# Masking attention blocks with an identity matmul and two exponentials instead of GpSimd selects, in a two-layer hybrid decoder

## The chip, the cores and the metric

The kernel runs on one core of one Trainium2 chip. The metric is the device time of one execution in microseconds (us); the time before is the median of three runs.

## The reference

Two layers are applied to a prompt group (one sequence of 1024 tokens) and to a sample group (8 sequences with 4 new tokens each, with cached keys and values). Layer 0 projects the input to queries, keys, values and gates; an attention A (window 128, with a sink) and an attention B (three head groups with dilations 1, 4 and 16, merged by their softmax denominators) follow; the result is multiplied by a SiLU gate, projected and normalised. Layer 1 is an mLSTM and takes no part in the change. Cut to the attention over blocks of 128 queries:

```python
def banded_attention(q, k, v, span, sink=None):
    ...
    s = jnp.einsum('nbqhgd,nbkhd->nbhgqk', qb, kk, preferred_element_type=F32)
    qi = jnp.arange(BLOCK)[:, None] + BLOCK
    ki = jnp.arange(2 * BLOCK)[None, :]
    dist = qi - ki
    band = (dist >= 0) & (dist <= span)
    ...
    p, den, lse = _softmax_stats(s, mask, sink_b)
    o = jnp.einsum('nbhgqk,nbkhd->nbqhgd', p, vv.astype(F32))

def layer0_prompt(x, w_in, sinks, w_out, ln_g, ln_b):
    ...
    oa, _ = banded_attention(qa, ka, va, A_WINDOW, sinks.reshape(A_KV_HEADS, A_GROUP))
    ...
    for g in range(N_B_GROUPS):
        win, dil = B_DILATIONS[g]
        o, lse = banded_attention(_to_sub(qb[:, :, g], dil), _to_sub(kb[:, :, g], dil),
                                  _to_sub(vb[:, :, g], dil), win // dil)
    ...
    y = _layer0_out(x, oa, obs, lses, z, w_out, ln_g, ln_b)
```

## The kernel before

Matrix products are made from pairs: a number is split into a rounded part (F32R, `hi`, a copy on ScalarE, L111) and the rest (`lo`, a subtraction on VectorE, L114), and a product is three matmuls. Layer 0 runs in stages: keys and values (`proj_kv`), queries of attention A, then query projections of B woven with attention A and the row maxima of B (`weave`, L941), then the gate projections `proj_z0` (tile `pj`, L199 to L201) woven with attention B (L964), then what is left of attention B woven with the sample attention and the merges (L984), then the output projection `out0` (tile `py`, L165 to L167) and layer 1.

`scores` (L450) handles one block of 128 queries of 4 heads against 128 keys, as a tile of 128 keys x 512. There are 100 such blocks: 30 in attention A, 35 for each of the two key heads of attention B. Two matmuls fill a PSUM bank `sc` (L462, L463; the second one takes the low part of the query and the negative row maximum); ScalarE writes p = exp(sc) (L465); GpSimd puts zeros where a key must not be seen (L468 to L476: one select for the own or the previous block, two selects and a memset for the group with dilation 16); ScalarE copies p to the rounded `ph` (L479, counted under L112), and `pl` = p - ph is made on VectorE (L483, counted under L116) or, for every fourth block outside of attention A, on GpSimd (L481). Three matmuls `av` (L485 to L487) add the block to the output, which VectorE takes out (L577 to L580). `Q1` and `Q2` are loaded for every 256 queries, and ScalarE copies 64 rows of `Q1` to `Q2` (L370).

Instructions are put in order by a scheduler that simulates the engines; `ahead` gives a stream priority. Tiles live in pools whose memory is used again after a release, and a tile that takes over memory waits for the last reader of what was there. Two pools matter here. `sm` (L913) holds small tiles of the attention, the mask `maskq` first; it is released at L970, before the remaining blocks of attention B (those after `EARLY` = 9 steps of the second key head, called the late attention here) are written out. `smt` (L982, 4 buffers) is opened after that release and holds the tiles `KT`: all cached keys and values of the sample attention, 24 loads. Its first buffer takes over memory that `sm` had. All these loads are issued by SyncE (SP), which works its queue off in order, as are the loads of the Q tiles, of the output weights (`wr<-in_wo`, L848) and of the merges (`mo`, `mf`, `mz`, L830 to L832). The sample attention makes scores `sS` (L681) from `KT`, then `so` (L728) from `KT` and the weights. The output projection adds its result to `xr` (L879), loaded at L874.

## Time and profile before

| what | value |
|---|---|
| median of three runs | 1497.61 us (1493.66 to 1716.2) |
| the profiled execution's own time | 1500.81 us |
| its span on the core | 1499.1 us |
| mean granted TensorE clock | 0.973 of full |
| busy TensorE (PE) | 1405.4 us, 94% |
| busy VectorE (DVE) | 901.5 us, 60% |
| busy ScalarE (ACT) | 515.1 us, 34% |
| busy GpSimd (POOL) | 276.0 us, 18% |

The rows come from the one profiled execution. A matmul's recorded duration overlaps with the next one's, so the distance of two starts is what a matmul costs in a row of them. A busy share is a mean over stages that have different limits; the stages are looked at by windows of time. "a <- b" after an idle time names what the engine waited for.

### The profile page before, as it was taken

The page shows a single profiled execution, that of the slowest core. Times are in us where ns is not written, and L with a number is a line of the kernel's source. Part 1 is how long each engine was busy: PE and PEld are TensorE (multiplying, and loading weights), DVE is VectorE, ACT ScalarE, POOL GpSimd, SP SyncE. Part 2 cuts the span into 40 slices and gives each one's busy share as a digit, 9 for nine tenths or more (in the row PEclk, how much of TensorE's full clock was granted, in tenths as well). Part 3 has the DMA queues.
Part 4 walks back from the last instruction along what each step waited for, and adds up shares of the span by engine and source line. Part 5 has one row for each costly group of instructions (what it writes and reads, how often), then busy time and mean ns, then how long its engine had stood idle before and what let it go on. Part 6 is the DMA issues. An engine that isn't in the chain of part 4 may idle for free.

```text
span 1499.1 us, 21984 instructions
## 1 busy us (share of the span) xinstructions
PE 1405.4 (94%) x7792; PEld 1191.7 (79%) x7792; DVE 901.5 (60%) x2479; ACT 515.1 (34%) x938; POOL 276.0 (18%) x351
## 2 busy tenths in 40 slices
PE   8999999998899778979999999999999999999997
PEld 7989999898898444458788878988898899877785
DVE  5411457578566858768764536655565565566786
ACT  5332244542123776621133313331333133333310
POOL 1002233422322866401000000100000000000010
PEclk9999999999999888989999999999999999999999
DMA  8445655556653766794212655354223312431731
GB/s 307 168 142 171 199 190 164 173 162 185 186 190 111 195 169 186 241 300 140 95 51 87 220 191 201 109 194 124 78 82 122 108 50 69 131 116 39 233 131 46
DMA packets 139307, 226.86 MB, mean 151 GB/s; under 512 B 17216, under 2 KB 107296, under 8 KB 138680
## 3 DMA queue, kind: packets, MB, share of 16 engines
q1 hardware_dynamic: 131134, 204.09, 44.5%
q10 hardware_dynamic: 8064, 21.37, 4.0%
q8 instruction: 62, 1.02, 0.3%
q14 instruction: 47, 0.39, 0.1%
HBM read 166.60 MB, written 81.88 MB: 166 GB/s over the span
## 4 chain that ended last, share of the span: by engine, by line
PE 69%; DMA 16%; DVE 8%; issue 3%; ACT 2%; POOL 2%; SPq 1%; DVEq 0%; ACTq 0%; POOLq 0%
PE pj L199 10%; PE pj L201 10%; PE pj L200 10%; PE py L165 4%; PE py L167 3%; PE py L166 3%; DMA G<-GR 3%; PE pvo L165 3%; PE pvo L166 3%; PE pvo L167 3%; DMA wr<-in_wo_dram 1%; PE st L433 1%; DMA QZ<-QQ 1%; DMA out_cmems_dram<-Cs 1%; PE sc L463 1%
## 5 line engine op out<-in xcount | busy, mean ns | idle before, releaser
L199 PE MATMUL pj<-xh,wh 128*128 128x384 f32 (+1 forms) x576 | 189.3, 329 | 8.1 <-DVE sz L613 3.6
L199 PE MATMUL pj<-x1h,wh 128*128 128x384 f32 (+1 forms) x576 | 189.5, 329 | 1.7 <-ACT QT L1152 1.6
L200 PE MATMUL pj<-xl,wh 128*128 128x384 f32 (+1 forms) x576 | 188.5, 327 | 0.0
L201 PE MATMUL pj<-xh,wl 128*128 128x384 f32 (+1 forms) x576 | 188.4, 327 | 0.0
L201 PE MATMUL pj<-x1h,wl 128*128 128x384 f32 (+1 forms) x576 | 187.6, 326 | 0.0
L200 PE MATMUL pj<-x1l,wh 128*128 128x384 f32 (+1 forms) x576 | 187.4, 325 | 0.0
L199 PEld LDWEIGHTS pj<-xh,wh 128*128 128x128 f32 x576 | 110.6, 192 | 12.7 <-DVE sz L613 4.5
L199 PEld LDWEIGHTS pj<-x1h,wh 128*128 128x128 f32 x576 | 108.5, 188 | 6.5 <-issue 3.3
L201 PEld LDWEIGHTS pj<-x1h,wl 128*128 128x128 f32 x576 | 108.4, 188 | 6.0 <-issue 5.8
L200 PEld LDWEIGHTS pj<-xl,wh 128*128 128x128 f32 x576 | 110.5, 192 | 1.6
L201 PEld LDWEIGHTS pj<-xh,wl 128*128 128x128 f32 x576 | 110.8, 192 | 1.1
L200 PEld LDWEIGHTS pj<-x1l,wh 128*128 128x128 f32 x576 | 108.5, 188 | 4.0 <-issue 3.8
L437 DVE CUSTOM_DVE_ANT_0 junk<-st,maskq 128x256 f32<-128x256 f32 (+1 forms) x256 | 93.1, 364 | 27.4 <-PE st L433 6.8
L165 PE MATMUL pvo<-voh,x1h 128*128 128x512 f32 x256 | 101.0, 397 | 2.6 <-DVE SZ L1168 2.6
L166 PE MATMUL pvo<-voh,x1l 128*128 128x512 f32 x256 | 100.3, 394 | 0.0
L167 PE MATMUL pvo<-vol,x1h 128*128 128x512 f32 x256 | 99.7, 393 | 0.0
L807 POOL TENSOR_TENSOR rsw<-rsw,mhalf 128x1 f32<-128x1 f32 (+1 forms) x54 | 40.0, 741 | 322.3 <-DVE rsw L806 306.6
L116 DVE TENSOR_TENSOR pl<-p,ph 128x512 fp32r<-128x512 f32 x82 | 67.0, 825 | 29.0 <-ACT ph L112 27.0
L122 POOL TENSOR_TENSOR wl<-wr,wh 128x1024 fp32r<-128x1024 f32 x24 | 57.9, 2414 | 130.1 <-ACT qs L233 69.9
L112 ACT ACTIVATE wh<-wr 128x1024 fp32r<-128x1024 f32 x48 | 50.7, 1056 | 73.9 <-PE pj L200 69.6
L112 ACT ACTIVATE ph<-p 128x512 fp32r<-128x512 f32 x100 | 60.7, 627 | 27.0 <-POOL p L474 9.3
L1198 POOL MEMSET V<- 128x2 f32 x64 | 4.3, 99 | 348.6 <-PE num L1327 213.9
(350 smaller groups left out, 3244.8 us busy)
## 6 DMA issues: line engine op xcount, KB each, us to landing
Q<-QQ SPq DMA_DIRECT2D x32, 512.0 KB
out_kvs_dram<-in_cache_b_kv_dram SPq DMA_DIRECT2D x16, 1022.0 KB
wr<-in_w0f_dram SPq DMA_DIRECT2D x24, 512.0 KB
wr<-in_w1f_dram SPq DMA_DIRECT2D x24, 512.0 KB
QQ<-sh ACTq DMA_DIRECT2D x16, 512.0 KB
QQ<-sl ACTq DMA_DIRECT2D x16, 512.0 KB
QZ<-QQ SPq DMA_DIRECT2D x32, 256.0 KB
wr<-in_wo_dram SPq DMA_DIRECT2D x16, 512.0 KB
```

The source lines that it names most:

```text
L112: return self.nc.scalar.activation(out, in_, AF.Copy, scale=scale)
L116: return self.nc.vector.tensor_tensor(out, in_, f(hi), OP.subtract)
L122: self.nc.gpsimd.tensor_tensor(out, in_, f(hi), OP.subtract)
L165: nc.tensor.matmul(ps, xh[:, k, t], wh, start=k == 0, stop=False)
L166: nc.tensor.matmul(ps, xl[:, k, t], wh, start=False, stop=False)
L167: nc.tensor.matmul(ps, xh[:, k, t], wl, start=False, stop=k == 7)
L199: nc.tensor.matmul(ps[:, :n], wh[:, k, :], xh[:, k, :n], start=k == 0, stop=False)
L200: nc.tensor.matmul(ps[:, :n], wh[:, k, :], xl[:, k, :n], start=False, stop=False)
L201: nc.tensor.matmul(ps[:, :n], wl[:, k, :], xh[:, k, :n], start=False, stop=k == 7)
L433: nc.tensor.matmul(st[:, u, :], Q1[:, h, q0:q0 + 128], K1[:, w0:w0 + 256], start=True, stop=True)
L437: nc.vector.tensor_tensor_reduce(junk[:, :n], st[:, u, c0:c0 + n], mk, 1.0, -3e38, OP.add, OP.max, ST[:, 8 * h + qb:8 * h + qb + 1])
L807: nc.gpsimd.tensor_tensor(r, v, self.mhalf[:m], OP.pow)
```

## The change

A block's scores get a third matmul, ahead of the others: the mask (128 x 128, rounded values) as weights against `ident4`, four identity matrices side by side, puts the mask into the bank, and the two others add to it. The selects and the memset on GpSimd are gone. ScalarE makes the exponential of the bank twice, once rounded to `ph` and once in full to `p`; the copy from p to ph is gone. `p` has 3 buffers in place of 4. The mask comes through a buffer of the weights and a rounding copy to `maskr`, and `ident4` is made once on VectorE; both lie in `sm`.

```diff
--- before.py
+++ after.py
@@ -459,24 +459,15 @@
                 self.nsc += 1
                 ks = slice(128 * kb, 128 * kb + 128)
                 so = sc.rearrange("p (h q) -> p h q", h=4)
-                nc.tensor.matmul(so, K1[:, ks], Q1[:, :, q0:q0 + 128], start=True, stop=False)
+                mk = self.maskr[:, 256:384] if g == 3 else self.maskr[:, 128 - 128 * kind:256 - 128 * kind]
+                nc.tensor.matmul(so, mk, self.ident4, start=True, stop=False)
+                nc.tensor.matmul(so, K1[:, ks], Q1[:, :, q0:q0 + 128], start=False, stop=False)
                 nc.tensor.matmul(so, K2[:, ks], Q2[:, :, q0:q0 + 128], start=False, stop=True)
-                p = self.ppool.tile([128, 512], F32, tag="p", name="p", bufs=4)
-                nc.scalar.activation(p, sc, AF.Exp)
-                if g == 3:
-                    pv = p.rearrange("p (h s q) -> p h s q", h=4, s=2)
-                    nc.gpsimd.affine_select(pv[:, :, 0, :], pv[:, :, 0, :], [[0, 4], [1, 64]], OP.is_ge, 0.0,
-                                            base=0, channel_multiplier=-1)
-                    nc.gpsimd.affine_select(pv[:, :, 1, :], pv[:, :, 1, :], [[0, 4], [1, 64]], OP.is_ge, 0.0,
-                                            base=64, channel_multiplier=-1)
-                    nc.gpsimd.memset(pv[0:64, :, 1, :], 0.0)
-                elif kind == 0:
-                    nc.gpsimd.affine_select(p, p, [[0, 4], [1, 128]], OP.is_ge, 0.0, base=0, channel_multiplier=-1)
-                else:
-                    nc.gpsimd.affine_select(p, p, [[0, 4], [-1, 128]], OP.is_ge, 0.0, base=0, channel_multiplier=1)
                 ph = self.ppool.tile([128, 512], F32R, tag="ph", name="ph")
                 pl = self.ppool.tile([128, 512], F32R, tag="pl", name="pl")
-                self.hi(ph, p)
+                p = self.ppool.tile([128, 512], F32, tag="p", name="p", bufs=3)
+                nc.scalar.activation(ph, sc, AF.Exp)
+                nc.scalar.activation(p, sc, AF.Exp)
                 if g and self.nsc % POOL_LO == 0:
                     nc.gpsimd.tensor_tensor(pl, p, f(ph), OP.subtract)
                 else:
@@ -911,8 +902,14 @@
                 tc.tile_pool(name="vp", bufs=2) as self.vp, tc.tile_pool(name="ppool", bufs=3) as self.ppool, \
                 tc.tile_pool(name="odp", bufs=1) as self.odp:
             sm = self.sm = tc.alloc_tile_pool(name="sm", bufs=1)
-            self.maskq = self.sm.tile([128, 384], F32, name="maskq")
-            self.load(self.maskq, A['maskq'])
+
+            raw = self.wraw.tile([128, 1024], F32, tag="wraw", name="mkr")
+            self.load(raw[:, 0:384], A['maskq'])
+            self.maskr = self.sm.tile([128, 384], F32R, name="maskr")
+            self.hi(self.maskr, raw[:, 0:384])
+            self.maskq = f(self.maskr)
+            self.ident4 = self.sm.tile([128, 4, 128], F32R, name="ident4")
+            nc.vector.tensor_copy(self.ident4, self.ident.unsqueeze(1).to_broadcast([128, 4, 128]))
             self.sinkb = self.sm.tile([128, 64], F32, name="sinkb")
             self.load(self.sinkb, A['sinkb'])
             self.sinkc = self.sm.tile([32, 2], F32, name="sinkc")
```

On SP's queue the first loads of the sample attention stood thus before, behind the loads for a part of the late attention (a name in brackets is the semaphore waited for: DMAHW of a DMA, PE, DVE, Activation and Pool of an engine; Q, K and V are the late attention's loads, `OD_92` its output):

```order
L106 DMA Q_5863<-QQ_77 128x4x256 [waits DMAHW0_49,PE_49]
L106 DMA Q_5865<-QQ_77 1x4x256 [waits DMAHW2_49,PE_49]
L109 DMA FD_95<-dn 32x128 [waits DVE_49]
L106 DMA KT<-in_kt_dram 128x512 [waits DMAHW7_49,DMAHW3_49,DMAHW2_49]
L106 DMA KT<-in_kt_dram 128x512 [waits DMAHW4_49]
L106 DMA KT<-in_vc_dram 128x512 [waits DMAHW5_49]
L106 DMA KT<-in_vc_dram 128x512 [waits DMAHW6_49]
L106 DMA mf<-FD_95 64x2x384
L106 DMA mf<-FD_95 64x2x384 [waits DMAHW0_49]
L106 DMA KT<-in_kt_dram 128x512 [waits DMAHW3_49,DMAHW1_49,PE_49]
L106 DMA V<-VV 128x8x128 [waits Pool_49]
L106 DMA KT<-in_kt_dram 128x512 [waits DMAHW4_49,PE_49]
```

and now they stand here, behind every load of the late attention and behind the store and the reload of a part of its result:

```order
L106 DMA Q_6181<-QQ_76 128x4x256 [waits DMAHW1_49,PE_49,Activation_49]
L106 DMA Q_6183<-QQ_76 1x4x256 [waits DMAHW2_49,PE_49]
L106 DMA Q_6310<-QQ_76 128x4x256 [waits DMAHW4_49,PE_49,Activation_49]
L106 DMA Q_6312<-QQ_76 1x4x256 [waits DMAHW5_49,PE_49]
L109 DMA OD_92<-OD 260x1x384 [waits DVE_49]
L106 DMA mo<-OD_92 64x2x384 [waits DMAHW3_49,DMAHW2_49,Pool_49]
L106 DMA mf<-OD_92 64x2x384
L106 DMA mo<-OD_92 64x2x384
L106 DMA mf<-OD_92 64x2x384 [waits DMAHW6_49]
L106 DMA KT<-in_kt_dram 128x512 [waits DMAHW7_49,PE_49]
L106 DMA KT<-in_kt_dram 128x512 [waits DMAHW0_49]
L106 DMA KT<-in_vc_dram 128x512 [waits DMAHW1_49]
```

The first `KT` load had waits for DMAs alone. Now it waits for PE, and the count it asks for is that of the last mask matmul of the late attention, since its buffer lies where `maskr` lay. The 23 others stand behind it.

On PE the first scores of the sample attention stood among the late attention's blocks:

```order
L485 MATMUL av<-ph,V 66x512 [waits DVE_49,PE_49]
L486 MATMUL av<-ph,V 64x512
L487 MATMUL av<-pl,V 66x512
L681 MATMUL sS<-KT,scrh 32x128 [waits DMAHW7_49,DMAHW3_49,DMAHW2_49]
L681 MATMUL sS<-KT,scrh 32x128 x3
L462 MATMUL sc<-Q_5803,K_5471 128x512 [waits Activation_49]
L463 MATMUL sc<-Q_5805,K_5472 128x512
L681 MATMUL sS<-KT,scrh 32x128 [waits DMAHW4_49]
L681 MATMUL sS<-KT,scrh 32x128 x3
L485 MATMUL av<-ph,V 66x512 [waits DVE_49,PE_49,Activation_49]
L486 MATMUL av<-ph,V 64x512
```

and now they follow the last block's scores (L463 to L465 are the mask's and the two old matmuls, L476 to L478 the `av` matmuls, L672 the sample's scores in the new numbering):

```order
L476 MATMUL av<-ph,V 66x512 [waits Activation_49]
L477 MATMUL av<-ph,V 64x512
L463 MATMUL sc<-ident_948,maskr 128x512 [waits PE_49,Activation_49]
L464 MATMUL sc<-Q_6310,K_5991 128x512
L465 MATMUL sc<-Q_6312,K_5992 128x512
L478 MATMUL av<-pl,V 66x512 [waits Pool_49]
L463 MATMUL sc<-ident_948,maskr 128x512 [waits PE_49,Activation_49]
L464 MATMUL sc<-Q_6310,K_5991 128x512
L465 MATMUL sc<-Q_6312,K_5992 128x512
L476 MATMUL av<-ph,V 66x512 [waits DVE_49,Activation_49]
L477 MATMUL av<-ph,V 64x512
L672 MATMUL sS<-KT,scrh 32x128 [waits DMAHW7_49,PE_49]
```

All of `sS` and `so` moved behind the last `sc`; on PE 96 of the 416 matmuls `py` of the output projection still stand ahead of the last `so`. From layer 1 on the order is the same.

## Rows read from the trace of the kernel before

**Rows 1.** The page, part 4: the chain that ended last, by engine.
```profile
PE 69%; DMA 16%; DVE 8%; issue 3%; ACT 2%; POOL 2%; SPq 1%; DVEq 0%; ACTq 0%; POOLq 0%
```
**Rows 2.** Windows, core 0: busy us by engine, granted clock, DMA share, GB/s.
```profile
core 0: us, PE busy (x) PEld busy (x) DVE busy (x) ACT busy (x) POOL busy (x), PEclk, DMA share, GB/s
185.00:330.00 145.00, 141.68 (x824) 130.71 (x823) 90.93 (x231) 70.16 (x117) 56.59 (x48) 0.99 0.53 165
470.00:580.00 110.00, 87.15 (x343) 54.29 (x342) 74.22 (x113) 77.38 (x126) 77.59 (x102) 0.86 0.64 177
580.00:625.00 45.00, 41.05 (x185) 19.62 (x183) 38.28 (x70) 30.97 (x60) 28.04 (x28) 0.96 0.78 246
640.00:660.00 20.00, 14.28 (x108) 10.36 (x108) 12.48 (x11) 3.75 (x6) 0.00 (x0) 0.91 0.99 310
645.00:680.00 35.00, 24.29 (x143) 18.45 (x143) 21.68 (x28) 9.92 (x12) 1.84 (x1) 0.85 0.88 267
```
**Rows 3.** Timeline of PE: 128x512 matmuls in a row, at 215 and at 672 us.
```profile
215.65 0.39 PE L462 MATMUL sc<-Q,K 128*128 128x512 f32 x1
215.88 0.40 PE L463 MATMUL sc<-Q,K 65*128 65x512 f32 x1
...
671.98 0.63 PE L165 MATMUL py<-oh,mh 128*128 128x512 f32 x1
672.40 0.63 PE L166 MATMUL py<-oh,ml 128*128 128x512 f32 x1
```
**Rows 4.** Groups by line and shape, whole span: busy us, mean ns, idle before.
```profile
L116 DVE TENSOR_TENSOR pl<-p,ph 128x512 fp32r<-128x512 f32 x82 | 67.0, 825 | 29.0 <-ACT ph L112 27.0 <-PE av L487 1.8
L112 ACT ACTIVATE ph<-p 128x512 fp32r<-128x512 f32 x100 | 60.7, 627 | 27.0 <-POOL p L474 9.3 <-PE av L486 8.8 <-POOL p L472 6.1
L465 ACT ACTIVATE p<-sc 128x512 f32<-128x512 f32 x100 | 56.1, 588 | 10.6 <-PE sc L463 6.2 <-POOL pl L481 2.3 <-DVE pl L116 1.7
L474 POOL TENSOR_SCALAR_AFFINE_SELECT p<-p 128x512 f32<-128x512 f32 x48 | 45.3, 947 | 40.4 <-ACT p L465 35.6 <-DVE pl L116 4.6
```
**Rows 5.** Windows of the exponentials alone (L465).
```profile
470.00:500.00 30.00, 6.02 (x11) 0.89 0.49 145
500.00:580.00 80.00, 21.37 (x38) 0.85 0.69 189
```
**Rows 6.** Tile sc, matmuls from 500 to 640 us: min/median/max ns, first and last start.
```profile
L463 PE MATMUL sc<-Q,K x56: 388/399/792, 501.0 to 623.2; 65*128 65x512 f32 x56
```
**Rows 7.** Tile pj, matmuls from 470 to 520 us.
```profile
L201 PE MATMUL pj<-xh,wl x28: 293/334/445, 469.8 to 496.4; 128*128 128x384 f32 x16, 128*128 128x288 f32 x12
```
**Rows 8.** Waits from 475 to 580 us: total, times, longest.
```profile
DVE pl L116 <- ACT ph L112: 15.5, 10, 6.3
...
POOL p L468 <- ACT p L465: 8.6, 5, 4.7
...
ACT ph L112 <- POOL p L472: 6.1, 4, 3.8
```
**Rows 9.** Groups from 500 to 580 us: the copies to Q2.
```profile
L370 ACT ACTIVATE Q<-Q 64x1024 fp32r<-64x1024 f32 x13 | 13.7, 1052 | 8.8 <-DMA Q<-QQ 8.8
```
**Rows 10.** Tile pl from 470 to 640 us: min/median/max ns.
```profile
L116 DVE TENSOR_TENSOR pl<-p,ph x52: 615/692/1527, 479.9 to 633.5; 128x512 fp32r<-128x512 f32 x52
```
**Rows 11.** Tile KT: last matmuls, and the issues of its loads on SP.
```profile
L728 PE MATMUL so<-KT,scrh x128: 269/273/425, 636.2 to 655.9; 128*32 128x128 f32 x128
...
L106 SPq DMA_DIRECT2D KT<-in_kt_dram x12: 328/346/588, 572.8 to 608.5; - x12
```
**Rows 12.** DMA view from 616 to 685 us: packets, MB, mean rate.
```profile
DMA packets 8157, 16.60 MB, mean 241 GB/s; under 512 B 795, under 2 KB 5209, under 8 KB 8153
```
**Rows 13.** DMA issues from 560 to 690 us: engine, op, count, KB each.
```profile
KT<-in_kt_dram SPq DMA_DIRECT2D x8, 512.0 KB
KT<-in_vc_dram SPq DMA_DIRECT2D x8, 512.0 KB
...
wr<-in_wo_dram SPq DMA_DIRECT2D x6, 512.0 KB
...
mz<-SZ SPq DMA_DIRECT2D x4, 288.0 KB
KT<-in_kt_dram SPq DMA_DIRECT2D x4, 256.0 KB
KT<-in_vc_dram SPq DMA_DIRECT2D x4, 256.0 KB
```
**Rows 14.** Chain from 560 to 700 us, in order of time: start, us, what.
```profile
631.47 3.06 DMA KT<-in_vc_dram
```
**Rows 15.** Timeline of DVE: the first L879, where the output projection is taken out.
```profile
680.76 2.48 DVE L879 SCALAR_TENSOR_TENSOR xr<-xr,py 128x512 f32<-128x512 f32 x4
```

## The prediction, made before the changed kernel had run

> **What bounds the kernel now.** I read the chain of waits first. It is 69% PE and 16% DMA, with ACT and POOL at 2% each [rows 1]: no engine that loses work here stands much on the path as a whole. So I went on by stages, with the windows [rows 2]. The reader is to see three. From 185 to 330 us, where attention A is woven into the projections, PE is busy 141.7 of 145 us at a granted clock of 0.99: PE sets the pace and POOL's selects are covered. From 470 to 580 us no engine is full: PE 87, DVE 74, ACT 77 and POOL 78 of 110 us. There attention B goes hand over hand, and the waits show it: POOL's select waits for ACT's exponential, ACT's copy waits for POOL, DVE's subtraction waits for the copy [rows 8]. From 640 to 680 us PE is free for a part of the time, and the DMA engines are busy 0.99 and then 0.88: the sample attention's last loads, the merges and the output weights are what everything waits for. Behind 680 us, where the output projection's results are first taken out [rows 15], both kernels have the same work in the same order. So the question is when that point comes in the changed kernel: what comes later there ends later.
>
> **Small parts.** The mask's way through a weight buffer, its rounding copy and the four identities are three instructions and a load while the projections run; I take 0. If they delayed a weight load the price is one load, 3.06 us by the nearest row [rows 14]; a gain is excluded, since nothing goes. The p tile with 3 buffers is made later and read once, by the subtraction; I take 0. A bank `sc` is now held by two exponentials. With two banks, a turn of one bank is three matmuls and two exponentials, 3 x 0.23 + 2 x 0.59 = 1.9 us for two blocks, or about 1 us a block, less than every pace used below; so 0, and if the waits between them doubled it, 2 us a block, the pace of before.
>
> **Stage of attention A.** A 128x512 matmul in a row costs 0.23 us at the full clock (2.4 GHz) and 0.43 us at the half (1.2 GHz) [rows 3]. 30 blocks get one each: 30 x 0.23 = 6.9 us on an engine that is the bound. What could give it back is PE's idle time, 145 - 141.7 = 3.3 us. I take 6.9; bounds 3.6 and 30 x 0.43 = 12.9.
>
> **Stage of attention B.** ACT loses a copy of 627 ns and gains an exponential of 588 ns [rows 4]: nothing. POOL loses a select of 947 ns a block [rows 4] that stood between the exponential and the copy. PE gains 0.23 us a block. Before, the last projection matmul is at 496.4 us [rows 7] with 11 blocks through [rows 5]; the other 59 take until 623.2 us [rows 6], 2.15 us each. In the changed order only 7 blocks come before that matmul, four fewer, which takes 4 x 5 x 0.23 = 4.6 us from PE ahead of it, and the 7 masks add 1.6. With the 6.9 of the stage before it comes at 496.4 + 6.9 - 4.6 + 1.6 = 500.3 us, with 63 blocks left.
>
> Their pace has a floor and a ceiling. ACT cannot go below 2 x 0.59 us for the exponentials plus the copies to Q2, 13.7 us for 38 blocks from 500 to 580 us [rows 5, 9] = 0.36 us, so 1.55 us. If what POOL gives back is eaten by the other hand-overs, it stays at 2.15. The chain of a block loses 0.95 us of 2.15, but two or three blocks are under way at once, so less than half of that shows. I take 1.8, near the middle. The last mask matmul comes at 500.3 + 63 x 1.8 = 614 us, 9 us earlier than the last scores before; bounds 598 (1.55) and 636 (2.15).
>
> **The new wait.** The order shows that the first KT load now waits for that last mask matmul, since its buffer lies over `maskr`. Before, the loads of the keys left from 572.8 to 608.5 us [rows 11], beside the late attention. Now 24 KT loads stand on SP behind this wait, and behind them (the queue is in order) six loads of the output weights, the loads of the last merges, the normalisation's weights, and the first `xr`. The bytes: KT 16 x 0.524 + 8 x 0.262 = 10.5 MB, output weights 6 x 0.524 = 3.1 [rows 13], merges 4.2 (8 tiles of 192 KB, 8 of 128, one `mz` of 384, 4 of 288), the rest 2.4, together 20.2, and one `xr` of 0.5: 20.7 MB. Who waits: `sS` and `so` on PE, all merges that need the sample's columns, and `py`, of which 96 of 416 matmuls stand ahead of the last `so`. Before, 96 were done as well when the results were first taken out: four in a row from 680.8 us on [rows 15], of 24 matmuls each; the last `so` had been at 655.9 [rows 11].
>
> The rate is the term that I know least. A mix of the same loads moved at 310 GB/s in its best stretch, with the DMA engines at 0.99; at 267 over 645 to 680 us [rows 2]; and at 241 over 616 to 685 us with its gaps [rows 12]. That is 67, 77.5 and 86 us. I take 267, the middle one, because the serial tail also has gaps: four buffers, and a wait of exponential and transposes between the keys and the values. With 3 us until the first load lands [rows 14], the first take-out is at 614 + 3 + 77.5 = 694.5 us.
>
> The Trainium skill, "DMA: Bandwidth & Descriptors", Specifications, gives about 358 GB/s as what one core gets from HBM. By it 20.7 MB would be an estimated 58 us and the first take-out at 675 us. The trace shows 310 GB/s with the engines at 0.99 busy, so with these loads the engines are full below that figure.
>
> **Sum.** 694.5 - 680.8 = 13.7 us later. On the profiled execution's 1500.8 us that is 1514.5. The median of the runs is 3.2 us below that execution, so 1511.
>
> **Rivals.**
> (1) POOL's silence pays more than I say, a little faster. For it: DVE's subtraction takes 615 ns at its shortest and 692 at the median in this stretch [rows 10] but 825 as a mean of all [rows 4], and POOL waits and makes wait at every block [rows 8]. Against it: ACT's floor. At 1.6 us a block the last mask is at 601, and at 310 GB/s the take-out is at 601 + 3 + 67 = 671, 9.8 us earlier: 1491 in the profile, 1488 as a median. Only below ACT's floor, or if the loads didn't wait, would it be faster by over 2%. The Trainium skill, "GPSIMD Engine Reference", section 1, says that GpSimd shares its SBUF interfaces with VectorE, with contention for VectorE instructions with two SBUF inputs. The gap between 615 and 825 agrees with it, but no row here shows that the selects are its cause.
> (2) The wait takes more than the whole gain: the first KT load's place in SP's queue is the bound. The late attention ends at 500.3 + 63 x 2.0 = 626, and the tail moves 241 GB/s, 86 us: 715 us, 34 later, 1535 in the profile, 1532 as a median. It decides from 711 us on (2% is 30 us, and about what a measurement of this kernel can tell from no change). For it: the sample attention has only that rate in a stretch where much of it ran alone. Against it: that stretch contains gaps made by the late attention's end.
> (3) PE is the new bound in attention B: it was granted 0.86 there [rows 2], and six matmuls at 0.43 us are 2.6 us a block. At 2.15 on the mean the last mask is at 636 and the take-out at 636 + 3 + 77.5 = 716.5, 35.7 later: 1536.5, as a median 1533. Against it: busier engines were granted 0.96 and 0.99 in other windows.
> (4) The change hides altogether: the late attention ends so early that the tail is as long as the gain, 681 us, 1501 and 1498 as a median. It lies inside the forecast's own spread.
>
> **How the numbers follow.** Forecast 0.53 (with its spread from 1498 to 1524), rival 1 0.19, rival 2 0.18, rival 3 0.06, rival 4 0.04. Faster by over 2% is 0.03, the end of rival 1. Slower by over 2% is rivals 2 and 3 as far as they pass 711 us, 0.20, and 0.03 of the forecast: 0.23. Within 2% is the rest, 0.74. The range goes from rival 1's 1488 to just above rival 3's 1533.
>
> **What would show it.** Right: no select on POOL; an ACT exponential pair of some 590 ns each; PE's `sc` start 30 x 0.23 us later behind the first stage; the first KT load issued only at the last mask matmul, near 614 us; DMA busy and PE half idle from then to some 695 us; the first L879 some 14 us later than before and everything behind it shifted by as much. Wrong: KT loads before 600 us would refute the wait; the last mask after 630 or before 600 the pace; a take-out 60 or 95 us behind the last mask the rate; a change of the time behind the take-out the claim that nothing differs there.

## The result, and the profile after

The changed kernel takes 1509.26 us, the median of four runs (1506.27 to 1510.51), against 1497.26 us before. The ratio is 1.0085, 95% interval 1.006 to 1.0111: slower by a little under 1%. Of the kernel before one execution of four took 1716.2 us, which counts in the median of 1497.26 us but not in the ratio. The prediction was 1511 us. The profiled execution took 1509.37 us, 8.6 us more than the one of before; that one lies 3.5 us above its kernel's median, so by medians the difference is 12.0 us.

The page of the changed kernel, part 1, and its chain by engine [rows 1]:

```profile
PE 1419.9 (94%) x7892; PEld 1205.5 (80%) x7892; DVE 891.0 (59%) x2480; ACT 511.7 (34%) x939; POOL 180.5 (12%) x219
...
PE 68%; DMA 17%; DVE 7%; issue 3%; ACT 2%; SPq 1%; POOL 1%; DVEq 0%; POOLq 0%; ACTq 0%
```

POOL lost 95 us of work and PE gained 14.5; POOL's share of the chain went from 2% to 1%, so little of the first was on the chain. The windows that answer to [rows 2], and those of the new tail:

```profile
core 0: us, PE busy (x) PEld busy (x) DVE busy (x) ACT busy (x) POOL busy (x), PEclk, DMA share, GB/s
185.00:330.00 145.00, 143.96 (x829) 131.12 (x829) 81.45 (x199) 67.48 (x114) 30.84 (x18) 1.00 0.50 159
400.00:470.00 70.00, 66.78 (x435) 65.61 (x436) 48.49 (x202) 15.20 (x25) 15.66 (x9) 1.00 0.52 155
470.00:580.00 110.00, 94.28 (x369) 60.59 (x367) 81.96 (x134) 80.16 (x135) 28.82 (x24) 0.89 0.62 178
605.00:625.00 20.00, 6.48 (x31) 2.51 (x29) 14.48 (x16) 3.13 (x6) 2.67 (x1) 0.65 0.61 174
625.00:680.00 55.00, 48.09 (x276) 28.68 (x276) 33.93 (x63) 17.32 (x37) 3.10 (x2) 0.87 0.93 287
650.00:660.00 10.00, 8.43 (x35) 3.67 (x33) 9.37 (x18) 1.74 (x2) 0.00 (x0) 1.00 1.04 380
605.00:690.00 85.00, 59.82 (x371) 34.70 (x369) 49.67 (x85) 22.34 (x47) 5.77 (x3) 0.80 0.81 251
```

From 185 to 330 us PE's idle time fell from 3.3 to 1.0 us. From 605 to 625 us PE does 6.5 us of work in 20, and is granted 0.65: it has run out of scores to make. Of its idle time there 2.7 us end with a load of the keys and 2.9 with a subtraction `pl`; the longest piece ends with a rounded output weight `oh`, for the first `py` (timeline of PE):

```profile
626.16 0.80 PE L165 MATMUL py<-oh,mh 128*128 128x512 f32 x1 [9.01 <-ACT oh L112]
```

From 625 to 680 us the DMA engines are busy 0.93.

The groups that answer to [rows 4]:

```profile
L470 ACT ACTIVATE p<-sc 128x512 f32<-128x512 f32 x100 | 59.4, 596 | 0.0
L469 ACT ACTIVATE ph<-sc 128x512 fp32r<-128x512 f32 x100 | 59.2, 593 | 38.9 <-PE sc L465 24.2 <-DVE pl L116 7.5 <-PE av L477 5.2
L116 DVE TENSOR_TENSOR pl<-p,ph 128x512 fp32r<-128x512 f32 x82 | 59.2, 733 | 20.9 <-ACT p L470 20.8
```

The two exponentials cost 593 and 596 ns, the exponential and the copy of before 588 and 627. VectorE's subtraction fell from 825 to 733 ns on the mean; e3 below shows that the selects' going is the smaller part of that. The last mask matmul, and below it the last projection matmul, which answers to [rows 7] (tiles sc and pj: min/median/max ns, first and last start):

```profile
L463 PE MATMUL sc<-ident,maskr x70: 387/397/632, 471.2 to 605.2; 128*128 128x512 f32 x70
```

```profile
L201 PE MATMUL pj<-xh,wl x13: 294/298/346, 470.1 to 480.7; 128*128 128x288 f32 x8, 128*128 128x384 f32 x5
```

And the tail on SP's queue, from the first KT load to the first `xr`, some of its rows (timeline: start, us, what):

```profile
605.70 1.65 SPq L106 DMA_DIRECT2D KT<-in_kt_dram  x2
607.39 0.91 SPq L106 DMA_DIRECT2D KT<-in_vc_dram  x2
...
635.74 1.31 SPq L106 DMA_DIRECT2D KT<-in_kt_dram  x3
...
666.34 0.38 SPq L106 DMA_DIRECT2D mz<-SZ  x1
670.66 7.70 SPq L106 DMA_DIRECT2D KT<-in_vc_dram  x6
686.46 1.28 SPq L106 DMA_DIRECT2D xr<-in_xtok_dram  x3
```

The first load leaves half a microsecond after the last mask matmul has started, the last ones some 70 us later, and the `xr` that the output projection's results need stands behind them. It leaves only after the last `so`, in this kernel as in all others here, and the 96 `py` ahead of it had started by 664.8 us (tiles KT and py):

```profile
L719 PE MATMUL so<-KT,scrh x128: 272/421/422, 672.6 to 686.0; 128*32 128x128 f32 x128
```

```profile
L167 PE MATMUL py<-ol,mh x32: 387/390/776, 630.5 to 664.8; 128*128 128x512 f32 x32
```

So the take-out, which before followed the last of its `py` (680.3 us), now follows the end of the sample attention. The first one (timeline of DVE; before: [rows 15]) is late:

```profile
690.00 1.29 DVE L870 SCALAR_TENSOR_TENSOR xr<-xr,py 128x512 f32<-128x512 f32 x2 [1.14 <-issue]
```

It comes 9.2 us later than before and the execution ends 8.6 us later; behind the take-out the two kernels take 820.0 and 819.4 us.

### The profile page after: what moved, and what is told of

Same layout as the page of the kernel before. It is cut to its first block, busy times and chain, and to the rows that moved or that the text cites. A ratio compares the mean times of both kernels' runs of the same rounds, so it can differ in the third digit from the quotient of the medians.

```text
span 1507.6 us, 22066 instructions
## 1 busy us (share of the span) xinstructions
PE 1419.9 (94%) x7892; PEld 1205.5 (80%) x7892; DVE 891.0 (59%) x2480; ACT 511.7 (34%) x939; POOL 180.5 (12%) x219
## 4 chain that ended last, share of the span: by engine, by line
PE 68%; DMA 17%; DVE 7%; issue 3%; ACT 2%; SPq 1%; POOL 1%; DVEq 0%; POOLq 0%; ACTq 0%
PE pj L199 10%; PE pj L201 10%; PE pj L200 10%; PE py L167 3%; PE py L165 3%; PE py L166 3%; PE pvo L165 3%; PE pvo L166 3%; PE pvo L167 3%; DMA G<-GR 3%; DMA wr<-in_wo_dram 2%; DMA QZ<-QQ 1%; DMA OD<-OD 1%; DMA out_cmems_dram<-Cs 1%; DMA Q<-QQ 1%
## 5 line engine op out<-in xcount | busy, mean ns | idle before, releaser
L199 PE MATMUL pj<-xh,wh 128*128 128x384 f32 (+1 forms) x576 | 186.4, 324 | 5.9 <-DVE sl L117 3.1
L199 PE MATMUL pj<-x1h,wh 128*128 128x384 f32 (+1 forms) x576 | 189.7, 329 | 1.7 <-ACT QT L1149 1.6
L201 PE MATMUL pj<-x1h,wl 128*128 128x384 f32 (+1 forms) x576 | 187.8, 326 | 0.0
L200 PE MATMUL pj<-x1l,wh 128*128 128x384 f32 (+1 forms) x576 | 187.6, 326 | 0.0
L201 PE MATMUL pj<-xh,wl 128*128 128x384 f32 (+1 forms) x576 | 185.6, 322 | 0.0
L200 PE MATMUL pj<-xl,wh 128*128 128x384 f32 (+1 forms) x576 | 185.4, 322 | 0.0
L199 PEld LDWEIGHTS pj<-xh,wh 128*128 128x128 f32 x576 | 108.2, 188 | 10.0 <-DVE sl L117 4.0
L199 PEld LDWEIGHTS pj<-x1h,wh 128*128 128x128 f32 x576 | 108.7, 189 | 6.5 <-issue 3.3
L201 PEld LDWEIGHTS pj<-x1h,wl 128*128 128x128 f32 x576 | 108.6, 188 | 6.0 <-issue 5.8
L200 PEld LDWEIGHTS pj<-x1l,wh 128*128 128x128 f32 x576 | 108.6, 189 | 4.0 <-issue 3.8
L201 PEld LDWEIGHTS pj<-xh,wl 128*128 128x128 f32 x576 | 108.2, 188 | 1.2
L200 PEld LDWEIGHTS pj<-xl,wh 128*128 128x128 f32 x576 | 108.2, 188 | 1.2
L437 DVE CUSTOM_DVE_ANT_0 junk<-st,maskr 128x256 f32<-128x256 f32 (+1 forms) x256 | 93.1, 364 | 23.6 <-PE st L433 9.8
L469 ACT ACTIVATE ph<-sc 128x512 fp32r<-128x512 f32 x100 | 59.2, 593 | 38.9 <-PE sc L465 24.2
L116 DVE TENSOR_TENSOR pl<-p,ph 128x512 fp32r<-128x512 f32 x82 | 59.2, 733 | 20.9 <-ACT p L470 20.8
L165 PE MATMUL py<-oh,mh 128*128 128x512 f32 x128 | 53.3, 416 | 12.3 <-ACT oh L112 9.0
```

What stands on the lines that cost most here:

```text
L116: return self.nc.vector.tensor_tensor(out, in_, f(hi), OP.subtract)
L165: nc.tensor.matmul(ps, xh[:, k, t], wh, start=k == 0, stop=False)
L199: nc.tensor.matmul(ps[:, :n], wh[:, k, :], xh[:, k, :n], start=k == 0, stop=False)
L200: nc.tensor.matmul(ps[:, :n], wh[:, k, :], xl[:, k, :n], start=False, stop=False)
L201: nc.tensor.matmul(ps[:, :n], wl[:, k, :], xh[:, k, :n], start=False, stop=k == 7)
L437: nc.vector.tensor_tensor_reduce(junk[:, :n], st[:, u, c0:c0 + n], mk, 1.0, -3e38, OP.add, OP.max, ST[:, 8 * h + qb:8 * h + qb + 1])
```

## The experiments

Twelve kernels ran. For each the table gives the median, the ratio to the kernel before with its interval, and from its one profiled execution the start of the last row maximum's matmul (`st`, the end of the first stage), of the last `sc` matmul, the first KT load, the last store of the late attention's output, the first take-out and the whole time. A ratio is taken against executions of the kernel before from the same session, with medians of 1497.3 us for the changed kernel, 1496.8 for e1 to e4, 1497.7 for e5 to e8 and 1499.2 for e9 to e12; across these groups the ratios are to be compared and not the medians. Places come from one execution each, and executions of one kernel differ: those of the kernel before range from 1490 to 1505 us.

| kernel | median | ratio (95%) | st | sc | KT | store | take-out | profiled |
|---|---|---|---|---|---|---|---|---|
| before | 1497.3 | 1 | 468.7 | 623.2 | 572.8 | 638.3 | 680.8 | 1500.8 |
| changed | 1509.3 | 1.0085 (1.006 to 1.0111) | 470.6 | 605.7 | 605.7 | 620.5 | 690.0 | 1509.4 |
| e1 | 1497.2 | 1.0003 (0.9978 to 1.0027) | 472.8 | 625.2 | 564.8 | 634.5 | 683.3 | 1501.4 |
| e2 | 1527.3 | 1.0192 (1.0157 to 1.0228) | 460.4 | 606.4 | 622.7 | 625.4 | 701.1 | 1521.8 |
| e3 | 1518.3 | 1.0132 (1.0098 to 1.0165) | 469.7 | 604.7 | 605.1 | 622.4 | 698.1 | 1519.1 |
| e4 | 1532.9 | 1.0233 (1.0205 to 1.0261) | 480.6 | 625.9 | 625.8 | 639.5 | 712.0 | 1532.7 |
| e5 | 1508.0 | 1.0075 (1.0052 to 1.0098) | 467.1 | 626.6 | 565.8 | 651.3 | 691.8 | 1509.3 |
| e6 | 1513.1 | 1.0111 (1.0087 to 1.0136) | 470.3 | 629.2 | 570.7 | 643.7 | 693.9 | 1511.3 |
| e7 | 1517.6 | 1.0137 (1.0109 to 1.0166) | 471.6 | 609.6 | 609.9 | 624.9 | 698.1 | 1518.7 |
| e8 | 1517.8 | 1.0154 (1.0119 to 1.0189) | 466.4 | 629.8 | 561.7 | 647.2 | 698.7 | 1514.3 |
| e9 | 1504.4 | 1.0043 (1.0026 to 1.006) | 469.0 | 627.1 | 567.4 | 634.5 | 686.9 | 1506.7 |
| e10 | 1504.7 | 1.0037 (1.0017 to 1.0058) | 470.3 | 628.9 | 566.9 | 638.8 | 687.7 | 1506.7 |
| e11 | 1506.2 | 1.0061 (1.0038 to 1.0085) | 466.0 | 620.2 | 554.9 | 634.3 | 685.1 | 1501.3 |
| e12 | 1497.6 | 0.9994 (0.9972 to 1.0015) | 469.4 | 619.2 | 560.7 | 629.2 | 677.4 | 1496.1 |

The last two columns differ by 816 to 821 us in all of them. So the take-out is the place at which these kernels part, as the prediction had it.

**e1: the wait taken away.** The mask and one rounded identity lie in a pool that outlives the late attention.

```diff
-            self.maskr = self.sm.tile([128, 384], F32R, name="maskr")
+            self.maskr = self.odp.tile([128, 384], F32R, name="maskr")
...
-            self.ident4 = self.sm.tile([128, 4, 128], F32R, name="ident4")
-            nc.vector.tensor_copy(self.ident4, self.ident.unsqueeze(1).to_broadcast([128, 4, 128]))
+            identr = self.odp.tile([128, 128], F32R, name="identr")
+            nc.vector.tensor_copy(identr, self.ident)
+            self.ident4 = identr.unsqueeze(1).to_broadcast([128, 4, 128])
```

> The changed kernel with the mask and the identity in a pool that lives until the late attention is done, so that no KT load waits for a mask matmul; one rounded identity is read four times by a repeating operand in place of four copies, because four copies leave no room for the KT tiles. Theory (the new wait eats the gain of attention B): the KT loads leave before 590 us again, the late attention ends near 610, the output projection's first take-out comes about 55 us behind it as in the kernel before, at 660 to 670 us, and the time is 1478 to 1490 us, faster than both kernels. Rival (the tail is bound by the bytes it moves, whenever the loads leave): the take-out stays within 5 us of 681 and the time is 1495 to 1503 us. Rival (the sample attention beside the late attention takes back what POOL gave): the late attention ends at 620 or later, 1493 to 1500 us.

Measured: 1497.2 us, 12 us below the changed kernel and level with the kernel before. The KT loads leave from 564.8 us on, so the wait is gone, and with it the whole loss. The theory's 1478 to 1490 us failed, and that e1 isn't faster than before is both rivals together. Beside the sample attention the late attention ends at 625 us again, and the windows fit that (from the start of attention B to the first KT load, and from there to the last scores):

```profile
473.00:565.00 92.00, 76.32 (x295) 48.36 (x294) 64.85 (x105) 66.01 (x111) 21.70 (x20) 0.91 0.63 183
565.00:625.00 60.00, 53.89 (x265) 29.44 (x265) 43.42 (x86) 40.28 (x84) 13.26 (x9) 0.97 0.74 224
```

PE is busy 0.83 of the first stretch and 0.90 of the second: where the two attentions run side by side PE is nearly full, as it was before (41.05 of 45 us from 580 to 625 us, [rows 2]), so relief for POOL can buy little there. And the tail from the last output store to the take-out took 48.8 us in place of 42.5.

**e2: the wait put into the kernel before.** 35 tiny operations on VectorE keep the old mask alive to the end of the late attention.

```diff
                 self.hi(ph, p)
+                if g and kv:
+                    one = self.ppool.tile([128, 1], F32, tag="one", name="one", bufs=1)
+                    nc.vector.tensor_tensor(one, f(ph)[:, 0:1], self.maskq[:, 0:1], OP.max)
```

> The kernel before, with selects and copies as they were, in which each late block of the second key head takes one column of the old mask into a maximum on VectorE that nobody reads (35 tiny operations): the first KT load then waits for the last of them, as it waits for the last mask matmul in the changed kernel. Theory: the late attention, alone on the engines, ends at 612 to 620 us, the tail takes some 85 us as in the changed kernel, the take-out is at 697 to 705, and the time is 1512 to 1524 us, slower than the changed kernel, since it has the wait without the faster attention. Rival (the wait costs nothing, the change's loss comes from the matmuls): 1496 to 1502 us.

Measured: 1527.3 us, 30 us above the kernel before and more than expected. The tile KT (matmuls and load issues; first and last start) shows the loads going out at 622.7 us and no earlier:

```profile
L684 PE MATMUL sS<-KT,scrh x32: 272/285/298, 627.6 to 651.2; 128*32 128x128 f32 x32
...
L106 SPq DMA_DIRECT2D KT<-in_kt_dram x12: 327/382/592, 622.7 to 662.1; - x12
```

That is 16 us behind its last scores at 606.4: the tiny maximum waits its turn on VectorE, behind the block's other work, where the mask matmul of the changed kernel is the first thing of its block. So e2 holds the loads longer than the change does. From the first KT load to the take-out it takes 78.4 us, the changed kernel 84.3. The wait alone, without any mask matmul, makes the kernel slower by more than the change does; the rival fell.

Three kernels of the table and the one of before also make a square for the last scores of attention B: with selects 623.2 us beside the sample attention (before) and 606.4 with it held back (e2); with the mask matmul 625.2 beside it (e1) and 605.7 with it held back (the changed kernel). So the new way by itself moved the last scores 2.0 us later in the one case and 0.7 earlier in the other, both small beside what executions of one kernel differ by. Counted from each kernel's last `st` the blocks of attention B take 154.5, 146.0, 152.4 and 135.1 us, which looks like a gain of 2 and of 11 us; but e2 has its last `st` 8 us before the kernel before, with the same code in attention A, and leaves 29 of the L201 projection matmuls behind it where the changed kernel leaves 12. Holding the sample attention back bought 17 to 20 us for attention B, and the price was a tail of 84 us in the open.

**e3: one exponential and the copy, with the mask matmul.**

```diff
-                nc.scalar.activation(ph, sc, AF.Exp)
                 nc.scalar.activation(p, sc, AF.Exp)
+                self.hi(ph, p)
```

> The changed kernel with one exponential and the rounding copy of before in place of the two exponentials; the mask matmul stays. Theory (a copy and an exponential cost ScalarE the same, 627 and 588 ns): the time stays within 5 us of the changed kernel, 1504 to 1514 us, with the last mask matmul at 603 to 610 us. Rival (the second exponential holds the PSUM bank and sets the pace of attention B): the last mask matmul 8 us or more earlier and 1495 to 1502 us.

Measured: 1518.3 us, 9 us above the changed kernel, outside the range. For the place of the last scores the theory holds, 604.7 us against 605.7; the loss is in the tail, 93.0 us from the first KT load. Some of its rows on SP (timeline) set beside those above:

```profile
661.25 0.92 SPq L106 DMA_DIRECT2D KT<-in_vc_dram  x2
...
676.72 0.38 SPq L106 DMA_DIRECT2D mz<-SZ  x1
677.19 10.57 SPq L106 DMA_DIRECT2D KT<-in_vc_dram  x6
```

The last six KT loads stand behind a load of the merges, `mz`, in both kernels; here that load leaves at 676.7 us in place of 666.3, and they leave 6.5 us later.

e3 has no selects either, so it tells apart what the selects and what the copy do. VectorE's subtraction (groups by line and shape) and the last projection matmuls (tile pj, from 400 us on):

```profile
L116 DVE TENSOR_TENSOR pl<-p,ph 128x512 fp32r<-128x512 f32 x82 | 63.6, 792 | 29.1 <-ACT ph L112 28.0 <-PE av L477 1.0
```

```profile
L201 PE MATMUL pj<-xh,wl x127: 288/334/522, 399.9 to 499.2; 128*128 128x384 f32 x80, 128*128 128x288 f32 x47
```

With the selects gone and the copy kept the subtraction takes 792 ns (785 in e10), between 825 and 733: some 35 ns of the fall go with the selects and some 55 with the copy. And the last projection matmul is at 499.2 us, near the 496.4 of before; the second exponential, and not the mask matmul, goes with its 480.7 in the changed kernel.

**e4: the mask matmul twice.**

```diff
                 nc.tensor.matmul(so, mk, self.ident4, start=True, stop=False)
+                nc.tensor.matmul(so, mk, self.ident4, start=False, stop=False)
```

> The changed kernel with the mask matmul made twice (the mask counts double, which changes nothing after the exponential). Theory: attention A is bound by PE and has no idle time left to take it up, so 30 x 0.23 = 6.9 us there; in attention B PE has idle time, 0 to 8 us there; 1514 to 1526 us. Rival (PE bounds attention B too): 100 x 0.23 = 23 us or more, 1530 us or later. Rival (PE is not the bound in either): under 3 us, 1508 to 1512 us.

Measured: 1532.9 us, 23.7 more than the changed kernel, 0.237 us for each of the 100 matmuls: the first rival by its time. The first stage ends at 480.6 us, 10.0 later, where the first 30 mask matmuls had cost 1.9; the last scores come 20.2 later, the tail is 1.9 longer and what lies behind it 1.3. PE's `st` and mask matmuls (tiles st and sc):

```profile
L433 PE MATMUL st<-K,QZ x256: 276/282/385, 172.4 to 480.6; 128*128 128x256 f32 x128
```

```profile
L464 PE MATMUL sc<-ident,maskr x70: 387/393/632, 482.1 to 625.4; 128*128 128x512 f32 x70
```

Up to the last scores a second mask matmul costs 0.20 us, nearly the 0.23 that it takes on PE. The first one cost nothing there: with the sample attention held back the last scores are at 606.4 us with selects (e2) and at 605.7 with the mask matmul. That fits a PE whose idle time the first one uses up, which e4 alone doesn't prove. How the 20.2 us divide between the two stages is not shown, since e4 leaves 32 of the L201 projection matmuls behind its last `st` and the changed kernel 12.

**e5 and e6: the new way in one part only.** e5 has it in the early blocks of attention B, e6 in attention A; elsewhere selects and copies of before. Each edit is a condition around the two versions of the lines in `scores`.

```diff
+                if g and (kv == 0 or g == 3):   # e5; e6: if g == 0:
+                    nc.tensor.matmul(so, mk, self.ident4, start=True, stop=False)
...
+                else:
+                    nc.tensor.matmul(so, K1[:, ks], Q1[:, :, q0:q0 + 128], start=True, stop=False)
...
```

> The mask matmul and the two exponentials only in the blocks of attention B that come before the late attention's main part (the first key head, and the group with dilation 16 of the second); selects and copies of before in attention A and in the other two groups of the second key head. So no KT load waits for the mask, and the stages in which PE is full (attention A, and the late attention beside the sample attention) get no matmul more. Theory (the new way gains only where PE has idle time and nothing waits for it): the last scores come 6 to 12 us before 623, the take-out 3 to 9 us before 681, 1487 to 1494 us. Rival (the tail from the late attention's outputs to the take-out is bound by what stands on SP and the gain is lost in it): 1495 to 1500 us.

> The mask matmul and the two exponentials in attention A alone; attention B with selects and copies as before (3 buffers of p). Theory: in attention A POOL's relief returns most of the 6.9 us of 30 matmuls, so the last row maximum comes 1 to 4 us later than at 468.7 and the time is 1498 to 1503 us. Rival (PE is the bound and nothing comes back): 1503 to 1507 us. Rival (it gains): below 1495 us.

Measured: e5 1508.0 us, e6 1513.1, both slower than the kernel before and later than theory and rivals allowed, though no KT load waits for a mask. In e6 the first stage ends at 470.3 us, 1.6 later than before, as the theory had it; in e5 at 467.1. What they lose comes later. In e5 the last output store, and on VectorE the merge ahead of the last accumulation and the take-out, are (timelines of SP and of DVE):

```profile
651.30 0.87 SPq L109 DMA_DIRECT2D OD<-OD  x1
```

```profile
645.56 4.96 DVE L849 RECIPROCAL mf<-mf 128x384 f32<-128x384 f32 x2 [4.02 <-DMA mf<-OD]
...
650.61 0.67 DVE L591 TENSOR_TENSOR OD<-av,OD 65x512 f32<-65x512 f32 x1
...
691.83 2.48 DVE L890 SCALAR_TENSOR_TENSOR xr<-xr,py 128x512 f32<-128x512 f32 x4
```

The last scores are at 626.6 us, 3.4 later than before, but the store is 13 later: the last accumulation of the output, at 650.61 us, stands on VectorE's queue behind two steps of a merge that wait for a reload of that same output. In e6 the last scores are 6 us later than before, and the tail is 50.1 us. e6 has 3 buffers of p with selects, where before had 4; whether its 6 us are due to that was not tried.

**e7 and e8: KT loads on GpSimd's queue.** e7 is the changed kernel with them, e8 is e5 with them.

```diff
-            self.load(t, src[:, s:s + 2])
+            self.nc.gpsimd.dma_start(t, src[:, s:s + 2])
```

> The changed kernel with the 24 KT loads issued by GpSimd, which is idle there, in place of SyncE; they still wait for the last mask matmul. Theory (the tail from the first KT load to the take-out, 84 us, is made by SP's order, where KT loads stand behind merges and output weights that wait for VectorE): the tail is 62 to 75 us and the time is 1487 to 1500 us. Rival (the bytes bound the tail): 80 us or more, 1505 to 1514 us.

> The mask matmul in the early blocks of attention B as in e5 and the KT loads issued by GpSimd as in e7. If both theories hold, the sample attention is no longer held up by SP's queue and the merges and output weights no longer by KT loads: take-out at 655 to 672 us, 1474 to 1490 us. If the selects on GpSimd and the loads behind them hold each other up: 1495 us or later.

Measured: 1517.6 and 1517.8 us; both theories fell. e7 has the tail of its rival but is 4 us later than the rival's range. e8 comes after 1495 us, as its text has it for selects and loads that hold each other up, but that they do so is not shown. In e7 the tail is 88.2 us, no shorter than on SP. The window from the first KT load to the take-out:

```profile
609.00:698.00 89.00, 62.61 (x371) 35.78 (x369) 49.23 (x84) 21.59 (x46) 18.51 (x27) 0.79 0.79 239
```

89 us at 239 GB/s are 21.3 MB, and the changed kernel's 85 us at 251 are 21.3 MB as well. The same bytes stand behind the wait in both, so this says what the tail moves and not what holds it; the DMA engines are busy 0.79 and 0.81 of it. What GpSimd's queue waited for in that window shows more:

```profile
POOL KT L660 <- PE sS L672: 23.7, 7, 6.9
POOL KT L655 <- PE sS L672: 8.3, 2, 6.5
POOL KT L660 <- PE so L719: 6.8, 4, 4.1
```

For 38.8 us a KT load waited for `sS` or `so` matmuls, which read one of the four `KT` buffers before it can be filled again. So leaving SP's queue didn't let the loads go earlier: they stand behind their own buffers. Merges on the same queue waited another 17.5 us. Whether more buffers would shorten the tail was not tried.

**e9 to e12: variants of e1.** e9 has attention A with selects (the mask matmul under `if g:`), e10 one exponential and the copy, e11 `EARLY = 3`, e12 a higher priority of the late attention.

```diff
-    EARLY = 9
+    EARLY = 3                                          # e11
...
-                weave((ahead(tc, self.late, AHEAD[2]), W3[0])
+                weave((ahead(tc, self.late, 400), W3[0])   # e12
```

> As e1 (mask and identity kept, no KT load waits), but attention A with selects and copies of before; all of attention B has the mask matmul and two exponentials. Theory (in attention A 30 matmuls cost PE more than POOL's relief gives back): the last row maximum is 3 to 6 us earlier than e1's 472.8, and the time 1489 to 1495 us. Rival (the tail's order decides, and changes with every version): outside of that by up to 10 us on either side although the last row maximum comes at 467 to 470.

> As e1, with one exponential and the rounding copy in place of two exponentials. Theory (copy and exponential cost ScalarE the same, and e3's 9 us came from the order of its tail): 1493 to 1502 us, the last scores within 4 us of e1's 625. Rival (the second exponential is worth 9 us by itself): 1503 us or later with the last scores later than 629.

> As e1, with EARLY = 3 in place of 9, so that the memory for the KT tiles is free six blocks earlier and more of the late attention runs beside the sample attention. Theory (the tail is bound by the bytes behind the first KT load, so earlier loads end earlier): the first KT load 6 to 12 us before e1's 564.8 and 1490 to 1496 us. Rival (PE is full where both attentions run, and the late attention's last output starts the tail): 1496 to 1504 us.

> As e1, with the late attention's priority in the scheduler raised from 60 to 400, above the sample attention's. Theory (the take-out follows the late attention's last output store by 40 to 50 us): the last output store comes 2 to 8 us before e1's 634.5, the take-out by as much, 1490 to 1496 us. Rival (the sample attention then ends later and takes the gain): 1497 us or later.

Measured: 1504.4, 1504.7, 1506.2 and 1497.6 us. e9's first stage ends 3.8 us before e1's, but its take-out is 3.6 us later, with 52.4 us from the last store to it: its rival. e10 has a ratio of 1.0037 where e1 has 1.0003, some 5 us more, with the last scores 3.7 us later: by its time its rival, by its place just within its theory. So the copy in place of the second exponential cost 9 us in e3 and 5 in e10, once in the tail and once for the most part before it; a quicker subtraction and earlier projections go with the second exponential, but that they are what makes it the better choice is not shown. e11 sends KT loads 10 us earlier and its profiled take-out is 1.8 us later than e1's: its rival by the place, while its median lies 2 us above the rival's range. e12 does what its theory says of the places, though its median is above the theory's 1496: the last store and the take-out of its profile are (SP, DVE)

```profile
629.24 0.86 SPq L109 DMA_DIRECT2D OD<-OD  x1
```

```profile
677.35 0.69 DVE L870 SCALAR_TENSOR_TENSOR xr<-xr,py 128x512 f32<-128x512 f32 x1
```

5.3 and 5.9 us before e1's. Its median is level with the kernel before (0.9994, 0.9972 to 1.0015), so no version here is faster than the kernel before.

## Why the prediction was right

It named the sign, the mechanism and nearly the size: 13.7 us of the profiled execution forecast, 8.6 measured, and 1511 against 1509.3 as a median. That it came so near is in part luck: the last projection matmul came 19.6 us before its forecast, the blocks behind it took 10.8 us longer and the tail 4.3, counted from the last mask matmul, so that three errors left the take-out 4.5 us early. Point by point:

- **The new wait.** Right, and shown from both sides. The first KT load left at 605.7 us with the last mask matmul; e1, without the wait, lost 12 us less; e2, with the wait alone, lost 30.
- **The tail's price.** 3 + 77.5 us forecast, 84.3 measured. The bytes were 20.7 MB by the order and are 21.3 by the window (85 us at 251 GB/s); the rate was taken as 267. Over five kernels with the wait the tail was 78 to 93 us, at mean rates of 235 to 263 GB/s; the prediction's bounds for it were 70 and 89 us with the first load's landing, so one of the five lies outside. The Trainium skill's figure of about 358 GB/s ("DMA: Bandwidth & Descriptors", Specifications) was not reached over the tail: the mean here was 251. From 650 to 660 us, though, the tail moved 380 GB/s, above that figure; so the 310 GB/s that the prediction read at full engines is a mean and no ceiling. The tail's 251 is 0.81 of 310, and 0.81 is the share of it in which the engines were busy: the rate term is idle time of the DMA engines, and e7 shows what the loads waited for in it.
- **Attention A.** Mis-sized: 6.9 us taken, bounds 3.6 to 12.9, measured 1.9 at the end of the row maxima. One pair of executions says little here: over the kernels of the table the last `st` lies at 460.4 to 469.0 us with selects in attention A (five kernels, mean 466.3) and at 466.0 to 472.8 with one mask matmul (eight, mean 470.1), so some 4 us. The idle time that could pay was larger than the 3.3 us that the prediction counted in one window. Another 70 us window, 400 to 470, went from 64.3 to 66.8 us of PE's work, with the granted clock from 0.95 to 1.00. e4 shows the other half: with 30 more matmuls the row maxima end 10.0 us later still, and with fewer projections done.
- **Start and pace of attention B.** Both off, with opposite signs. The last projection matmul was forecast at 500.3 us and came at 480.7; the blocks behind it were forecast at 1.8 us and took (605.2 - 480.7) / 64 = 1.95. The last mask matmul was then at 605.2 in place of 614. The step that failed is the start: it moved the old place of that matmul by counting blocks, while the projections had got further by 470 us: 13 of their L201 matmuls were left where [rows 7] has 28, so with L199 and L200 some 45 more were done. Behind it stands the term "nothing" for an exponential in place of a copy: with one mask matmul a block, or none, and a copy in attention A the last projection matmul is at 488 to 500 us (before, e2, e3, e5, e8, e9, e10), with two exponentials there at 476 to 483 (the changed kernel, e1, e6, e7, e11, e12). The last scores hardly move by it, 604.7 us in e3 and 605.7 in the changed kernel, with 14 and 6 blocks ahead of that matmul. So start and pace missed in opposite directions: more projections done early leave more blocks behind them.
- **What lies behind the take-out.** Right: 820.0 and 819.4 us.
- **Rival 1** needed a pace of 1.6; even with the selects gone it was 1.95. The subtraction, which reads two tiles in SBUF, did become quicker, 733 ns from 825, and 792 of e3 puts some 35 ns of that down to the selects. That part agrees with the contention between GpSimd and VectorE that the Trainium skill states ("GPSIMD Engine Reference", section 1). It changed little: VectorE is busy 82 of 110 us from 470 to 580 us. **Rival 2** needed a last mask matmul at 626 and a tail at 241 GB/s; the tail had 251, the mask came too early for it. **Rival 3**, PE as the bound of attention B, was given 0.06. It didn't come, since the blocks took 1.95 us and not 2.15; but e4 says that PE has little more to give: 100 further matmuls moved the last scores by 0.20 us each, though PE's window shows 94 of 110 us.

What is shown: the wait makes the kernel slower, by 30 us when it alone is put into the kernel before (e2), and without it the changed kernel is level with before (e1). That it costs just 12 us in the changed kernel is less sure: every version has an order of its own, and without the wait e5, e6 and e9 to e12 lie from level to some 16 us above the kernel before. What is argued: that e1 gains nothing since PE is nearly full beside the sample attention; e4 and the square of e1, e2 and the two kernels speak for it. What stays open: how much of the 40 to 52 us from the last output store to the take-out, in the kernels without the wait, is order and how much is bytes. It changed by up to 12 us between versions whose merges and output weights are the same.

## What to carry to other kernels

When a constant gets a new reader late in the program, look at what its memory is used for next: a tile that is released early and read late holds back whatever takes its place, here 10 MB of loads. Before an engine's work is moved, see who is full where it goes: 95 us taken off GpSimd, against 100 matmuls on PE, moved the last scores by 0.7 us where attention B ran alone and not forward at all where the sample attention ran beside it. And with a scheduler that orders everything anew, a change of a few microseconds is judged by several places that all versions share (here the last row maximum, the last scores, the last store and the first take-out), since the tail alone moved the time by as much from one version to the next.

## What the runs showed that was not expected

- Up to the last scores PE took up 100 mask matmuls for nothing in place of the selects (605.7 us against e2's 606.4), and the next 100 cost 20.2 us (e4), although PE had been busy 0.98 at a granted clock of 0.99 from 185 to 330 us before.
- Replacing a copy of 627 ns with an exponential of 593 ns, which looks like nothing, goes with a subtraction that is some 55 ns quicker and with some 18 us at the last projection matmul (e3 and e10 against the changed kernel and e1).
- The DMA issue of a KT load takes GpSimd 527 to 736 ns, by the tile KT of e7 (527 to 591 for the 16 loads of 512 KB, at L660), and SP 327 to 330 in most of the changed kernel's; the tail of e7 is 4 us longer.

```profile
L660 POOL DMA_DIRECT2D KT<-in_kt_dram x8: 527/529/591, 627.3 to 654.1; - x8
```
